# A two-layer encoder trunk: a copy goes ahead of a sigmoid in the first gate, and a weight's remainder goes behind the rotated rows in the heads

## The chip, the core and the metric

The kernel runs on one core of a Trainium2 chip. It is one program for five engines that each work through their own list in order: TensorE (PE, with its weight loads shown apart as PEld), VectorE (DVE), ScalarE (ACT), GpSimd (POOL) and SyncE (SP), which here does nothing but start DMA transfers. The engines meet only at semaphores. The metric is the device time of one launch in microseconds (us); lower is better.

## What is computed

Two layers over 512 tokens of width 1024. Layer 0 mixes tokens by neighbourhood attention, layer 1 by latent attention with a rotated key; after each mixer a gate is added that reads a per-layer embedding `p`:

```python
for i in range(DEPTH):
    xn = rmsnorm(x, norm_g[i])
    y = mixer_na(xn, ...) if i % 2 == 0 else mixer_mla(xn, ...)
    h = x + y
    gate = jax.nn.sigmoid(rmsnorm(h, ple_norm[i]) @ ple_w_gate[i])
    x = h + gate * (p[i] @ ple_w_proj[i])
return rmsnorm(x, final_norm)
```

In the latent attention a query has 64 plain and 32 rotated columns for each of 16 heads, and the scores are a plain product over all 96. All of it is float32.

## The kernel before

A float32 product is made of three products of two parts: each operand is split into a rounded part (`hi`, a copy on ACT that rounds) and a remainder (`lo`, a subtraction on DVE or POOL), and hi·hi, lo·hi and hi·lo are added in one PSUM bank. So each weight costs a load by SP, a cast on ACT and a subtraction on POOL (`load_w`, from line 70). A load takes one of three buffers `wraw`, and it can't start before the subtraction that last read that buffer is done.

**The gate of a layer** (`gate_seven`) is a 2x2 block product by seven products instead of eight, in the order 1, 7, 2, 6, 5, 3, 4 on TensorE. Each product has two halves `i` of 12 matmuls. Products 1, 7 and 6 open banks of their own (tags mm, S, T); 2 is added onto the bank of 1, products 5 and 3 onto the bank of 6, and 4 onto the bank of 7. Before product 5 writes on a bank of product 6, the sum of product 6 that stands there has to be copied out (`s6[i]`, line 649). The remainder of product 4's weight is prepared (`prep`, line 570) after the second of these copies. When a quarter of the gate is ready, `finish` (line 590) takes the sigmoid on ACT in place in the bank, multiplies by the embedding `pe` and adds to the residual `r` on DVE, and `done` (line 1052) takes the sum of squares of that half row on ACT. When both halves of 128 rows are there, `done` normalises them on DVE (`x1n`, line 1071), TensorE turns them (`ps_T`, three banks of tag T), and they are split again, `x1h` on ACT and `x1l` on DVE, into the input of layer 1. A bank of tag T is free for the next turn when both have read it.

**The heads of layer 1** (`mla_heads`) run as 64 rounds, 8 for each pair of heads `j`. A round has a score (`ps_S`, three matmuls of queries and keys), a row maximum on DVE (`mx`), an exponential on ACT, a reciprocal on DVE (`rc`), and the division of the row on POOL (`ex`, line 830). Three rounds later TensorE turns `ex` and it is split into `pt_hi` and `pt_lo`. Between the scores, `pieces(j)` puts the work for later pairs, a few matmuls at a time. For every second pair, `rope` makes 128 rows of rotated queries: its rounded part `rh` on ACT (line 771) and its remainder `rl` on POOL (line 772). SP then moves them, 32 rows at a time, into the query tiles `qe` and `qo` of the next two pairs (`move`, line 101); the third matmul of a score multiplies with the remainders, so it needs the moves of `rl`. In the odd pairs `pieces` also loads a weight (line 885): the next rotary weight in pairs 1 and 3, the embedding `p` of layer 1 (`pT`) in pair 5.

The order on each engine is set by a scheduler that runs ahead of time; `issue_after(x)` adds an edge on `x`'s own engine, so that what the block issues on that engine stands behind `x` there. It puts no semaphore.

Of the kernel before, what the change touches and what calls it, by code (L numbers as in the profile page):

```python
# [40 lines left out]
class Trunk:  # L41
# [522 lines left out]
    def gate_seven(self, pool, layer, rh, res, after):  # L564
# [4 lines left out]
        W, A, Bk, s1, s17, s6 = {}, {}, {}, {}, {}, {}  # L569
# [15 lines left out]
                    nc.gpsimd.tensor_tensor(out=lo[:, o], in0=raw[:, o], in1=hi[:, o].bitcast(F32), op=ALU.subtract)  # L585
                W[p].append((hi, lo))

        behind, loaded = [], self.last_load

        def finish(t, n, ps, o=0, wd=S, last=False):  # L590
            x = ps
# [27 lines left out]
        for k, p in enumerate(order):  # L619
            if k in (1, 2):  # L620
                prep(order[k + 3])
            if p == 7:
                self.mixed(5)
            if p == 6:
                self.mixed(3)
            x = self.X[p]
            for i in range(2):
                for o, wd in halves if i and p in (7, 4) else ((0, S),):
                    c = slice(o, o + wd)
                    if p in banks:  # L630
                        C[p, i, o] = self.psum("O" if o else banks[p])[:, :wd]
                    ps = C[home.get(p, p), i, o]
                    m = [(x[:, 2 * s + i, k * P:(k + 1) * P], W[p][k // 2][r][:, k % 2 * S + o:k % 2 * S + o + wd])
                         for c in range(2) for s, r in ((0, 0), (1, 0), (0, 1)) for k in (2 * c, 2 * c + 1)]
                    for j, (l, r) in enumerate(m):
                        with self.tc.issue_after(mm.ins):
                            mm = nc.tensor.matmul(ps, l, r, start=j == 0 and p in banks,  # L637
                                                  stop=j == 11 and p in (2, 3, 4), skip_group_check=True)
                    if p == 1:
                        s1[i] = self.temp("s1")  # L640
                        nc.scalar.activation(s1[i], ps, AF.Copy)
                    elif p == 7:
                        nc.vector.tensor_tensor(out=ps, in0=ps, in1=s1[i][:, c], op=ALU.add)
                        if o == 0:
                            s17[i] = self.temp("s17")
                        nc.scalar.activation(s17[i][:, c], ps, AF.Copy)
                    elif p == 6:
                        s6[i] = self.temp("s6")
                        copy = nc.scalar.activation(s6[i], ps, AF.Copy)
                        if i:  # L650
                            prep(order[-1], copy)
                        for (a, b, o), t in C.items():
                            if (a, b) == (7, i):
                                sub(t, t, s6[i][:, o:o + t.shape[1]])
                    elif p == 5:
                        q = self.psum("mm" if i else "T")
                        sub(q, ps, s17[i])
                        sub(ps, ps, s1[i])
                        finish(2 + i, 1, q, last=layer == 0)
                    elif p == 2:  # L660
                        finish(i, 0, ps, last=True)
                    elif p == 3:
                        finish(i, 1, ps, last=True)
                    else:
                        finish(2 + i, 0, ps, o, wd, True)
# [51 lines left out]
    def mla_heads(self, pool, xT, cT, sets, oT):  # L717


        nc, a = self.nc, self.a  # L720
# [6 lines left out]
        R, V, W_, A, PS = {}, {}, {}, {}, {}  # L727
# [14 lines left out]
            W = lambda s, k: w[s][:, o + k * P:o + (k + 1) * P]  # L742
            return [(W(r, k), (ch, cl)[s][:, 3 + k, :]) for s, r in ((0, 0), (1, 0), (0, 1)) for k in range(2)]

        def load(key, ap, n, after=None):

            with self.tc.issue_after((A.get(after) or self.last_copy).ins) if after else nullcontext():
                W_[key] = self.load_w(ap, n, parts=2)

        def load_qr(g, after=None):  # L750
            load(("qr", g), a["mla_qr"][g], 384, after)

        def load_kv(g, after=None):
            load(("kv", g), a["mla_kv"][g], 1024, after)
# [101 lines left out]
        def pieces(j):  # L856

            n, g = j + 1, j // 2 + 1
            w = [[] for i in range(8)]
            add = lambda i, f, *x: w[i].append(lambda: f(*x))  # L860
# [13 lines left out]
            if j % 2 == 0 and j < 6:  # L874
                add(4, load_qn, g, ("k", n))
                add(5, rope, g, 0, 1)
                add(6, rope, g, 1, 5)
                add(7, rope, g, 5, 9)
                add(7, load_kv, g, ("r", g))
            elif j == 6:  # L880
                add(4, load, "w0", a["proj"][1, 0], 1024, ("q", n))
                add(6, ple)
                add(7, ple)
            elif j < 7:
                add(2, *((load_qr, g + 1, ("q", n)) if j < 5 else (load, "p", a["pT"][1], 1024, ("q", n))))
                for t in range(NT):
                    add(6 + t // 2, values, g, t)
            else:
                add(0, load, "w1", a["proj"][1, 1], 1024, "latest")
                for i in (0, 1, 2, 3, 3, 4, 5, 6, 7, 7):  # L890
                    add(i, ple)
# [20 lines left out]

        zs = self.z_phase(a["mla_z"], xT, range(NEARLY))
        load_qr(0)
        late = []
        W_["kv", 0] = self.load_w(a["mla_kv"][0], 1024, parts=2, rest=nc.vector, late=late)
# [8 lines left out]
        for i in range(70):  # L925
# [13 lines left out]
            if i == 53:  # L939
                last = self.last_mm  # L940
# [279 lines left out]
```

## Time and profile before

| what | value |
|---|---|
| median of 3 runs | 660.94 us (660.82 to 661.03) |
| the profiled execution | 660.64 us, of which the span from first to last instruction is 658.4 us |
| TensorE matmuls | 647.0 us busy, 98% of the span |
| TensorE weight loads (overlap the matmuls) | 550.6 us, 84% |
| ACT | 439.1 us, 67% |
| POOL | 432.7 us, 66% |
| DVE | 402.1 us, 61% |
| mean granted TensorE clock | 0.995 |

All times on the time axis are from the start of the span. In the timeline a row has a start, a duration, the engine, the line of the kernel, the operation and its tiles; "[0.61 <-ACT s L649]" means that the engine was idle for 0.61 us before it, until ACT finished `s` of line 649. Matmuls are pipelined, so a row's duration overlaps the next one's: the distance between starts is the pace. The first gate lies at about 294 to 322 us, the heads at about 408 to 560 us.

### The profile page before, as it was taken

The numbers are of one execution on the slowest core, as the hardware profiler recorded it, in microseconds if no ns is written. First come the engines' busy times: TensorE is split into PE (matmuls) and PEld (weight loads), VectorE is DVE, ScalarE is ACT, GpSimd is POOL, SyncE is SP. The second block draws the span as 40 slices with busy tenths as digits, with TensorE's granted clock in tenths as the row PEclk, the third lists the DMA queues.
The fourth block names the chain that finished last, engine by engine and source line by source line (L and its number), as shares of the span: only waits on it lengthen the run. The fifth ranks groups of instructions, "written<-read, shape, count | busy, mean of one in ns | idle before, by whom it ended". The sixth has DMA issues, their size and how long they took to land.

```text
span 658.4 us, 10122 instructions
## 1 busy us (share of the span) xinstructions
PE 647.0 (98%) x3419; PEld 550.6 (84%) x3419; DVE 402.1 (61%) x856; ACT 439.1 (67%) x875; POOL 432.7 (66%) x381
## 2 busy tenths in 40 slices
PE   9999999999999999999999999999999999999994
PEld 6888888998988888887899888888888888888884
DVE  6290365845656516568834613888888886474855
ACT  7672586767767743787543635897979897537945
POOL 0495475895685673787554526785959878436974
PEclk9999999999999999999999999999999999999998
DMA  9944354987575989444733334120212213583524
GB/s 320 354 143 147 98 198 122 250 221 166 190 175 181 199 192 348 157 155 158 246 86 118 103 102 148 53 76 6 64 52 66 66 65 128 205 306 128 171 86 159
DMA packets 44755, 102.18 MB, mean 155 GB/s; under 512 B 4640, under 2 KB 17696, under 8 KB 44704
## 3 DMA queue, kind: packets, MB, share of 16 engines
q1 hardware_dynamic: 33776, 83.97, 38.0%
q0 software_dynamic: 10496, 16.78, 11.7%
q10 hardware_dynamic: 432, 0.79, 0.3%
q8 instruction: 27, 0.44, 0.3%
q14 instruction: 24, 0.20, 0.1%
HBM read 89.99 MB, written 25.17 MB: 175 GB/s over the span
## 4 chain that ended last, share of the span: by engine, by line
PE 92%; DVE 2%; ACT 2%; DMA 1%; issue 1%; POOL 1%; POOLq 0%; ACTq 0%
PE ps_mm L107 35%; PE ps_S L107 13%; PE ps_mm L734 7%; PE ps_T L139 6%; PE ps_O L845 5%; PE ps_T L637 4%; PE ps_T L107 3%; PE ps_O L107 3%; PE ps_T L238 2%; PE ps_O L400 2%; PE ps_S L637 2%; PE ps_mm L637 2%; PE ps_mm L184 2%; PE ps_T L388 2%; PE ps_S L352 1%; PE ps_S L351 1%
## 5 line engine op out<-in xcount | busy, mean ns | idle before, releaser
L84 POOL TENSOR_TENSOR wwlo<-wraw,wwhi 128x1024 fp32r<-128x1024 f32 (+5 forms) x78 | 143.3, 1852 | 74.7 <-ACT wwhi L83 53.2
L83 ACT ACTIVATE wwhi<-wraw 128x1024 fp32r<-128x1024 f32 (+5 forms) x81 | 65.5, 832 | 57.3 <-issue 19.2
L585 POOL TENSOR_TENSOR wlo<-wraw,whi 128x512 fp32r<-128x512 f32 x56 | 74.0, 1356 | 24.7 <-ACT whi L583 14.9
L830 POOL TENSOR_TENSOR ex<-ex,rc 128x512 f32<-128x512 f32 x64 | 66.1, 1043 | 25.1 <-DVE rc L829 18.1
L828 ACT ACTIVATE ex<-ps_S,mx 128x512 f32<-128x512 f32 x64 | 44.0, 687 | 12.1 <-DVE mx L826 11.1
L826 DVE TENSOR_REDUCE mx<-ps_S 128x1 f32<-128x512 f32 x64 | 43.7, 682 | 7.1 <-PE ps_S L107 6.5
L96 DVE TENSOR_TENSOR pt_lo<-ps_T,pt_hi 128x512 fp32r<-128x512 f32 x64 | 43.2, 681 | 7.6 <-ACT pt_hi L94 7.3
L374 POOL TENSOR_TENSOR ex<-ex,rc 128x128 f32<-128x128 f32 (+1 forms) x64 | 36.0, 619 | 15.0 <-DVE rc L370 15.0
L94 ACT ACTIVATE pt_hi<-ps_T 128x512 fp32r<-128x512 f32 x64 | 37.7, 594 | 4.2 <-PE ps_T L139 3.9
L107 PE MATMUL ps_mm<-xh,wwhi 128*128 128x512 f32 x152 | 40.3, 398 | 0.0
L107 PE MATMUL ps_mm<-xl,wwhi 128*128 128x512 f32 x152 | 38.4, 391 | 0.0
L139 PE MATMUL ps_T<-ident,ex 128*128 128x128 f32 x256 | 38.4, 272 | 0.0
L107 PE MATMUL ps_mm<-xh,wwlo 128*128 128x512 f32 x152 | 38.2, 391 | 0.0
L139 PEld LDWEIGHTS ps_T<-ident,ex 128*128 128x128 f32 x256 | 31.4, 140 | 7.7 <-POOL ex L830 0.4
L107 PEld LDWEIGHTS ps_mm<-xh,wwlo 128*128 128x128 f32 x152 | 28.3, 188 | 5.9
L107 PEld LDWEIGHTS ps_mm<-xl,wwhi 128*128 128x128 f32 x152 | 28.3, 188 | 5.7
L583 ACT ACTIVATE whi<-wraw 128x1024 fp32r<-128x1024 f32 x28 | 29.2, 1055 | 4.9 <-DMA wraw<-sum 2.7
L205 DVE TENSOR_TENSOR u<-ps_O,u 64x512 f32<-64x512 f32 x32 | 22.0, 687 | 17.2 <-ACT u L204 16.7
L368 ACT ACTIVATE ex<-ex,mx 128x128 f32<-128x128 f32 (+1 forms) x64 | 30.3, 476 | 2.7 <-DVE mx L358 1.8
L209 POOL TENSOR_TENSOR u<-u,z 128x512 f32<-128x512 f32 x16 | 21.9, 1368 | 15.2 <-DVE u L205 10.0
L107 PEld LDWEIGHTS ps_mm<-xh,wwhi 128*128 128x128 f32 x152 | 27.3, 188 | 4.8
L107 PE MATMUL ps_S<-ke,qe 96*128 96x512 f32 x96 | 29.0, 408 | 0.3 <-DMA qe<-rl 0.3
(432 smaller groups left out, 1847.0 us busy)
## 6 DMA issues: line engine op xcount, KB each, us to landing
sum<-gate POOLq DMA_DIRECT2D x12, 1024.0 KB, 8.2
wraw<-na_qk SPq DMA_DIRECT2D x16, 512.0 KB, 3.3
wraw<-sum SPq DMA_DIRECT2D x16, 512.0 KB, 3.3
pe<-pe SPq DMA_DIRECT2D x31, 256.0 KB, 6.4
wraw<-gate SPq DMA_DIRECT2D x12, 512.0 KB, 3.3
wraw<-na_v SPq DMA_DIRECT2D x8, 512.0 KB, 4.1
sum<-sum POOLq DMA_DIRECT2D x4, 1024.0 KB, 10.7
wraw<-na_o SPq DMA_DIRECT2D x8, 512.0 KB, 4.4
```

The costliest lines, as they stand in the source:

```text
L83: nc.scalar.activation(hi[:, c], raw[:, c], AF.Copy)
L84: f = lambda e, c=c: e.tensor_tensor(out=lo[:, c], in0=raw[:, c], in1=hi[:, c].bitcast(F32), op=ALU.subtract)
L94: self.last_copy = nc.scalar.activation(hi, src, AF.Copy, scale=scale)
L96: nc.vector.tensor_tensor(out=lo, in0=src, in1=hi.bitcast(F32), op=ALU.subtract)
L107: last = self.last_mm = nc.tensor.matmul(out, l, r, start=i == 0, stop=i == n - 1)
L139: self.last_mm = self.nc.tensor.transpose(t[:, i * P:(i + 1) * P], b, self.ident)
L585: nc.gpsimd.tensor_tensor(out=lo[:, o], in0=raw[:, o], in1=hi[:, o].bitcast(F32), op=ALU.subtract)
L637: mm = nc.tensor.matmul(ps, l, r, start=j == 0 and p in banks, stop=j == 11 and p in (2, 3, 4), skip_group_check=True)
L734: self.last_mm = nc.tensor.matmul(PS[key], *terms[i], start=i == 0, stop=i == len(terms) - 1)
L826: nc.vector.reduce_max(mx, sp, axis=AX.X, negate=True)
L828: nc.scalar.activation(ex, sp, AF.Exp, bias=mx, accum_out=sm)
L830: nc.gpsimd.tensor_tensor(out=ex, in0=ex, in1=rc.to_broadcast([P, S]), op=ALU.mult)
```

## The change

Two places. In the gate of layer 0 only, the second half of product 2 is no longer finished where it is computed; it is held back until the first copy of product 6 has been issued, and its `finish` is put behind that copy. In the heads, the three loads of the odd pairs get a second edge: what they issue on POOL (the weight's two subtractions) is put behind the remainder `rl` of the rotated rows of the same group.

```diff
@@ gate_seven
-        behind, loaded = [], self.last_load
+        behind, held, loaded = [], [], self.last_load
...
                     elif p == 6:
                         s6[i] = self.temp("s6")
                         copy = nc.scalar.activation(s6[i], ps, AF.Copy)
+                        if held:
+                            with self.tc.issue_after(copy.ins):
+                                finish(*held.pop(), last=True)
...
+                    elif p == 2 and i and layer == 0:
+                        held.append((i, 0, ps))
                     elif p == 2:
                         finish(i, 0, ps, last=True)
@@ mla_heads
-        def load(key, ap, n, after=None):
+        def load(key, ap, n, after=None, rests=None):
             with self.tc.issue_after((A.get(after) or self.last_copy).ins) if after else nullcontext():
-                W_[key] = self.load_w(ap, n, parts=2)
-
-        def load_qr(g, after=None):
-            load(("qr", g), a["mla_qr"][g], 384, after)
+                with self.tc.issue_after(A[rests].ins) if rests else nullcontext():
+                    W_[key] = self.load_w(ap, n, parts=2)
+
+        def load_qr(g, after=None, rests=None):
+            load(("qr", g), a["mla_qr"][g], 384, after, rests)
...
-                add(2, *((load_qr, g + 1, ("q", n)) if j < 5 else (load, "p", a["pT"][1], 1024, ("q", n))))
+                add(2, *((load_qr, g + 1, ("q", n), ("rl", g)) if j < 5 else
+                         (load, "p", a["pT"][1], 1024, ("q", n), ("rl", g))))
```

TensorE's list is the same in both, row for row. The first place is ACT's list in the first gate (`X_` is an operand of product 3, `s_` with L649 the copies of product 6, L592 a sigmoid, L1057 the sum of squares, L583 the casts of product 4's weight). Before:

```order
L646 ACTIVATE s_3177<-ps_S 128x512
L592 ACTIVATE ps_mm<-ps_mm,rs 128x512
L533 ACTIVATE X_3232<-b 128x512
L592 ACTIVATE ps_mm<-ps_mm,rs 128x512
L1057 ACTIVATE sq,ss<-r 128x512
L649 ACTIVATE s_3250<-ps_T 128x512
L649 ACTIVATE s_3266<-ps_T 128x512
L583 ACTIVATE whi<-wraw 128x1024 x2
```

And now:

```order
L646 ACTIVATE s_3177<-ps_S 128x512
L592 ACTIVATE ps_mm<-ps_mm,rs 128x512
L533 ACTIVATE X_3222<-b 128x512
L649 ACTIVATE s_3240<-ps_T 128x512
L592 ACTIVATE ps_mm<-ps_mm,rs 128x512
L1064 ACTIVATE sq,ss<-r 128x512
L649 ACTIVATE s_3266<-ps_T 128x512
L583 ACTIVATE whi<-wraw 128x1024 x2
```

The first copy has moved ahead of the second sigmoid and of the sum of squares; the second copy and the casts stand where they stood. On DVE the subtraction that uses the first copy moved with it, ahead of that sigmoid's product.

The second place is POOL's list in the heads, around the remainder `rl` of the last rotated rows (L772 before, L778 now; L84 is a weight's subtraction, here of `pT`). Before:

```order
L770 TENSOR_TENSOR rl<-rh,rl 128x512
L830 TENSOR_TENSOR ex<-ex,rc 128x512
L84 TENSOR_TENSOR wwlo<-wraw,wwhi 128x512 x2
L830 TENSOR_TENSOR ex<-ex,rc 128x512 x2
L772 TENSOR_TENSOR rl<-rl,rh 128x512
L830 TENSOR_TENSOR ex<-ex,rc 128x512
```

And now:

```order
L776 TENSOR_TENSOR rl<-rh,rl 128x512
L836 TENSOR_TENSOR ex<-ex,rc 128x512 x3
L778 TENSOR_TENSOR rl<-rl,rh 128x512
L84 TENSOR_TENSOR wwlo<-wraw,wwhi 128x512 x2
L836 TENSOR_TENSOR ex<-ex,rc 128x512
L209 TENSOR_TENSOR u<-u,z 128x512
```

The two subtractions of `pT` went from two places ahead of `rl` to right behind it. The same happened with the rotary weight of pair 3 (two subtractions of 128x192); the one of pair 1 stood behind its `rl` already and stays.

The third place is SP's list for the same rotated rows (3520 to 3523 are the tiles of the next pair, 3528 to 3531 of the pair after). Before:

```order
L101 DMA qe_3520<-rh 32x512
L101 DMA qo_3522<-rh 32x512
L101 DMA qe_3528<-rh 32x512
L82 DMA wraw<-mla_o 128x1024
L101 DMA qo_3530<-rh 32x512
L101 DMA qe_3521<-rl 32x512
L101 DMA qo_3523<-rl 32x512
```

And now:

```order
L101 DMA qe_3520<-rh 32x512
L101 DMA qo_3522<-rh 32x512
L101 DMA qe_3528<-rh 32x512
L101 DMA qe_3521<-rl 32x512
L101 DMA qo_3523<-rl 32x512
L101 DMA qe_3529<-rl 32x512
L101 DMA qo_3530<-rh 32x512
```

The moves of the remainder for the next pair now come ahead of the first load of the output weight `mla_o` and of a move for the pair after. The load of `pT` itself, which SP issued ahead of five moves of the rotated rows before, now stands behind them.

## The prediction

> **What bounds the kernel now.** I read the page's first part, then what TensorE waited for, then the timeline around each wait.
>
> ```profile
> PE 647.0 (98%) x3419; PEld 550.6 (84%) x3419; DVE 402.1 (61%) x856; ACT 439.1 (67%) x875; POOL 432.7 (66%) x381
> PE ps_T L637 <- ACT s L649: 0.6, 1, 0.6
> PE ps_mm L107 <- ACT x1h L94: 0.4, 1, 0.4
> PE ps_S L107 <- DMA qe<-rl: 0.3, 1, 0.3
> PEld ps_S L107 <- DMA qe<-rl: 1.0, 2, 0.8
> PEld ps_T L139 <- POOL ex L830: 0.4, 1, 0.4
> ```
>
> TensorE sets the end: 98% of the span, and no other engine above 67%. Time can be won only where TensorE stands, and the waits by engine name three such places of any size in the middle of the kernel. The change goes for the first (the copy of product 6) and the third (the moves of `rl`). It takes no matmul away. So the most that it can give is the length of these stands, and idle time in a row is less than that, because a matmul's duration covers part of the gap behind it; I measure from start to start.
>
> **First gate: what is removed.**
>
> ```profile
> 301.08 0.61 PE L637 MATMUL ps_T<-wlo,X 128*128 128x512 f32 x2
> 303.53 1.07 PE L637 MATMUL ps_T<-whi,X 128*128 128x512 f32 x4
> 304.43 0.61 PE L637 MATMUL ps_T<-wlo,X 128*128 128x512 f32 x2
> 305.66 1.20 PE L637 MATMUL ps_T<-whi,X 128*128 128x512 f32 x4 [0.61 <-ACT s L649]
> 306.69 0.62 PE L637 MATMUL ps_T<-wlo,X 128*128 128x512 f32 x2
> 303.07 0.63 ACT L533 ACTIVATE X<-b 128x512 fp32r<-128x512 f32 x1 [0.32 <-DVE b L557]
> 303.61 0.64 ACT L592 ACTIVATE ps_mm<-ps_mm,rs 128x512 f32<-128x512 f32 x1
> 304.40 0.63 ACT L1057 ACTIVATE sq<-r 128x512 f32<-128x512 f32 x1
> 305.03 1.06 ACT L649 ACTIVATE s<-ps_T 128x512 f32<-128x512 f32 x2
> ```
>
> Four matmuls take 304.43 - 303.53 = 0.90 us, 0.225 each. After the pair at 304.43 the next should start at 304.88; it starts at 305.66, 0.78 late. It also starts with no weight loaded ahead: its group of four takes 306.69 - 305.66 = 1.03 instead of 0.90, another 0.13. The stand costs **0.91 us**. The bank that it waits for was full at 301.69 (the row of 301.08 and its 0.61), but ACT took the cast at 303.07, the sigmoid of product 2 and a sum of squares first. In the new list the copy follows the cast: it takes the sigmoid's slot at 303.61 and, at half of 1.06, ends by about 304.2. That is 0.7 ahead of 304.88. Product 5's weight is split by then: POOL had nothing left to do for 3.25 us before 307.17, so all weights up to product 3's were done by 303.92 (that row stands below). So nothing takes the place of this wait there.
>
> What is late next on ACT: the held sigmoid starts about 0.5 later, the sum of squares 0.3 later, and DVE takes the subtraction of the copy before the sigmoid's product. Neither reaches TensorE: product 5 has two halves of 12 x 0.225 = 2.7 us each, and the second needs only the second copy, near 305.9.
>
> **First gate: what is given back.** The lead of 0.91 has to survive the passage into layer 1, where the normalised rows come from a chain that does not hang on TensorE alone.
>
> ```profile
> 307.17 5.05 POOL L585 TENSOR_TENSOR wlo<-wraw,whi 128x512 fp32r<-128x512 f32 x4 [3.25 <-issue]
> 312.25 0.33 SPq L82 DMA_DIRECT2D wraw<-mla_c  x1
> 314.15 0.66 ACT L592 ACTIVATE ps_T<-ps_T,rs 128x512 f32<-128x512 f32 x1 [0.37 <-PE ps_T L637]
> 314.74 0.62 ACT L1057 ACTIVATE sq<-r 128x512 f32<-128x512 f32 x1
> 315.81 0.85 ACT L83 ACTIVATE wwhi<-wraw 128x768 fp32r<-128x768 f32 x1 [0.36 <-DMA wraw<-mla_c]
> 321.40 1.41 DVE L1071 SCALAR_TENSOR_TENSOR x1n<-r,rs,gn 128x512 f32<-128x512 f32 x2
> 323.92 1.28 DVE L96 TENSOR_TENSOR x1l<-ps_T,x1h 128x512 fp32r<-128x512 f32 x2
> 322.12 1.47 PE L139 MATMUL ps_T<-ident,x1n 128*128 128x128 f32 x12
> 324.97 0.60 PE L139 MATMUL ps_T<-ident,x1n 128*128 128x128 f32 x4
> ```
>
> Read from the top: POOL ends product 4's subtractions at 312.22, which frees a load buffer; SP issues a load of layer 1's weight at 312.25; ACT waits for it until 315.81. Everything behind that cast on ACT, and through it on DVE (`x1n` at 321.40, `x1l` at 323.92), keeps its time although TensorE is earlier. This chain starts with the casts of product 4's weight, behind the second copy. With ACT's own distances (copy 0.53, half of 1.06; sigmoid 0.59, from 314.15 to 314.74; sum of squares 0.63, from 304.40 to 305.03) the second copy starts at 303.61 + 0.53 + 0.59 + 0.63 = 305.36, where it was 305.03 + 0.53 = 305.56. So the chain gains 0.20, against TensorE's 0.91.
>
> TensorE reaches the first turns at 322.12 - 0.91 = 321.21. Their third block needs `x1n` of the second row block, first half ready at 321.40 + 0.70 - 0.20 = 321.90; TensorE wants it after eight turns, at about 322.1: in time, barely. The next four turns, at 324.97 before, would come at 324.06, but they reuse the first of three tag-T banks, which DVE reads for `x1l` until 323.92 + 0.64 - 0.20 = 324.36. So TensorE stands again, for **0.30**. The bounds are 0 (the load lands early, or the chain moves along) and 0.65 (the load lands 0.3 later, because the embedding's load, tied to TensorE, moves toward it). I take the worked-out value, since each piece of it has a row.
>
> Net of this place: 0.91 - 0.30 = 0.61, between 0.26 and 0.91.
>
> **Heads: what is removed.**
>
> ```profile
> 515.34 0.94 PE L107 MATMUL ps_S<-ko,qo 128*128 128x512 f32 x3
> 516.12 0.65 PE L107 MATMUL ps_mm<-wwhi,cT 128*128 128x256 f32 x4
> 517.91 0.71 PE L107 MATMUL ps_S<-ke,qe 96*128 96x512 f32 x2
> 518.97 0.50 PE L107 MATMUL ps_S<-ke,qe 96*128 96x512 f32 x1 [0.34 <-DMA qe<-rl]
> 519.30 0.40 PE L734 MATMUL ps_mm<-cT,wwhi 128*128 128x512 f32 x1
> 509.37 1.03 POOL L830 TENSOR_TENSOR ex<-ex,rc 128x512 f32<-128x512 f32 x1
> 510.37 2.55 POOL L84 TENSOR_TENSOR wwlo<-wraw,wwhi 128x512 fp32r<-128x512 f32 x2
> 512.88 2.04 POOL L830 TENSOR_TENSOR ex<-ex,rc 128x512 f32<-128x512 f32 x2
> 514.87 1.30 POOL L772 TENSOR_TENSOR rl<-rl,rh 128x512 fp32r<-128x512 f32 x1
> 514.89 0.53 SPq L82 DMA_DIRECT2D wraw<-mla_o  x1
> 516.69 0.54 SPq L101 DMA_DIRECT2D qe<-rl  x1
> DMA to landing us min/median/max: 1.9/2.0/2.2
> 511.68 0.14 DVE L829 RECIPROCAL rc<-sm 128x1 f32<-128x1 f32 x1
> 511.94 0.63 ACT L771 ACTIVATE rh<-rl 128x512 fp32r<-128x512 f32 x1
> ```
>
> A score behind turns takes 516.12 - 515.34 = 0.78 to the next matmul; the one at 517.91 takes 519.30 - 517.91 = 1.39. The stand costs **0.61 us**. The move that it waits for was issued at 516.69, behind a remainder that POOL finished at 516.17 and behind a load and a move on SP.
>
> Now POOL does `ex`, `ex` and `rl` without the 2.55 between them. The second of these `ex` waits for `rc` (511.82), so it ends near 512.9; `rh` is ready at 512.57; `rl` runs from 512.9 to 514.2 instead of 514.87 to 516.17. On SP its move now follows the three moves of `rh`, the last of which was through at 514.8 (the load behind it went at 514.89). It is issued near 514.9, 1.8 earlier, and lands 2.0 later at 516.9; the third matmul wants it near 518.4. The wait is gone with 1.5 to spare, and 1 if the landing is a half slower. I take the full 0.61.
>
> What is paid: the 2.55 now lie behind `rl`, until 516.75, and the next `ex`, which followed the old `rl` at about 516.15, starts 0.6 later and ends near 517.8. Its turns are due at about 518.9 once the stand is gone, so 1.1 us cover it. `pT` itself is first used six rounds into pair 6, which begins with the score at 517.91, and the load buffer that it frees goes to an output weight, which is used when the heads end. So its later remainder and its later load cost nothing; without that cover they would cost up to the 2.55.
>
> **Small ones.** The weight load waited for `rl` a second time (1.0 less 0.8 = 0.2), at the rotated rows before these, where `rl` also moves ahead of two small subtractions; and a turn waited for `ex` (0.4 of PEld time), in a stretch where the new list has one `ex` ahead of the gate's product. Bounds 0 and 0.3; I take 0.14, about half.
>
> **The sum.** 0.61 + 0.61 + 0.14 = 1.36. The profiled execution was 660.64: 659.28. It lies 0.30 under the median of 660.94, so for a median **659.6 us**, 0.2% less.
>
> One page speaks for more. The Trainium skill, "TensorE: Matmul & The Clock Gate", section "A second HAM failure mode: psum-queue depth-cycling", holds that frequent short idling between groups makes TensorE's clock drop and be earned again, so a stand would cost more than its length. The trace does not bear it out:
>
> ```profile
> 304.00:307.00 3.00, 2.39 (x11) 1.67 (x10) 3.00 (x7) 2.85 (x7) 0.00 (x0) 1.00 0.60 175
> 508.00:523.00 15.00, 14.65 (x90) 12.53 (x89) 12.51 (x25) 12.71 (x28) 14.67 (x14) 1.00 0.25 72
> ```
>
> These are the busy times of PE, PEld, DVE, ACT and POOL in the two stretches with the stands; the granted clock is 1.00 in both.
>
> **The rivals.**
>
> *Nothing is given back* in the passage: 0.91 + 0.61 + 0.14 = 1.66, so 659.3. For it: DVE and ACT have gaps there. Against it: the cast at 315.81 waits for a load, not for TensorE.
>
> *More is given back, or one stand stays.* With the bound 0.65 of the passage and nothing from the small ones, 0.26 + 0.61 = 0.87: 660.1. If instead the move of `rl` still came late (SP's list stuck behind the earlier moves), 0.61 + 0.14 = 0.75: 660.2. That is the case in which the second half of the change does not do what it says; POOL's and SP's new lists speak against it.
>
> *Slower.* POOL was busy 14.67 of 15 us from 508 to 523. `rl` now stands ahead of `pT`'s work and waits for `rh` from ACT; if `rh` comes late, POOL stands, and every `ex` behind it, now with 2.55 of subtractions in front, is late too. The cover is 0.33 (512.9 less 512.57) before `rl` slips and then 1.1 before TensorE does. From about 1.4 late it costs TensorE one for one; at 3.9 late, 2.5 us, which turns 1.36 into -1.1: 662.1. Against it: `rh` stands where it stood on ACT, and nothing ahead of it there is later.
>
> **How the numbers follow.** Forecast 659.6: 0.50. Nothing given back, 659.3: 0.18. More given back or a stand left, 660.1 to 660.2: 0.24. Slower, about 662: 0.08. What this kernel's measurement can tell from no change is about 0.2%, 1.32 us, or 659.62: the forecast sits on that edge, so I split it in halves. Faster: 0.25 + 0.18 + 0.03 (a small part of the third) = 0.46; slower 0.08; the same 0.46. The range: 659.0 (all bounds good: 0.91 + 0.61 + 0.30 = 1.82, so 659.1, and 0.1 of the runs' spread) to 660.6 (0.26 and 0.14 with the second stand left, 0.40: 660.54). The slower rival and a little more stay outside.
>
> **What would show it.** TensorE's waits lose the rows for `s` of line 649 and for `qe<-rl`; the first matmul of product 5 follows within 0.3 us of the last of product 6. In the passage a wait of the turns for `x1l` of about 0.3 appears, and the cast behind the load of `mla_c` stays at its time less 0.2. `rl` of the last rows starts some 1.9 us ahead of the place it had, measured from the score before it. Wrong would be: a wait for `ex` in 515 to 525, a third cast whose load lands later, or a lead that is gone before the heads begin.

## The result, and the profile after

| | before | after |
|---|---|---|
| median | 660.94 us (660.81 to 661.04, 7 runs) | 658.66 us (658.40 to 659.07, 7 runs) |
| the profiled execution | 660.64 us | 658.60 us |
| its span | 658.4 us | 656.6 us |

The change makes the kernel faster by 2.28 us: the ratio is 0.9966, with a 95% interval of 0.9954 to 0.9978, so the gain is 1.5 to 3.0 us. The forecast was a gain of 1.36 us, to 659.6, in a range that began at 659.0. The direction was right, and the gain was larger than the range allowed.

The engines' busy times, and waits of PE and PEld (the weight loads) in the kernel after (us in total, times, longest):

```profile
PE 646.7 (98%) x3419; PEld 550.9 (84%) x3419; DVE 401.1 (61%) x856; ACT 439.3 (67%) x875; POOL 433.0 (66%) x381
PE ps_mm L107 <- ACT x1h L94: 0.4, 1, 0.4
PEld ps_mm L107 <- ACT x1h L94: 0.9, 2, 0.7
PEld ps_T L139 <- DVE x1l L96: 0.8, 2, 0.4
```

The rows for `s` of line 649 and for `qe<-rl` are gone, and so are PEld's for the two `ex`. Behind the first weights one row has grown: the turns wait for `x1l` twice now (0.8), where it was once (0.4). That is the place where the prediction gave 0.30 back.

The first gate, on PE and ACT (start, duration, engine and line, operation):

```profile
303.37 1.08 PE L637 MATMUL ps_T<-whi,X 128*128 128x512 f32 x4
304.28 0.61 PE L637 MATMUL ps_T<-wlo,X 128*128 128x512 f32 x2
304.74 1.07 PE L637 MATMUL ps_T<-whi,X 128*128 128x512 f32 x4
305.64 0.61 PE L637 MATMUL ps_T<-wlo,X 128*128 128x512 f32 x2
303.44 0.58 ACT L649 ACTIVATE s<-ps_T 128x512 f32<-128x512 f32 x1
303.92 0.65 ACT L592 ACTIVATE ps_mm<-ps_mm,rs 128x512 f32<-128x512 f32 x1
304.48 0.63 ACT L1064 ACTIVATE sq<-r 128x512 f32<-128x512 f32 x1
305.10 0.60 ACT L649 ACTIVATE s<-ps_T 128x512 f32<-128x512 f32 x1
```

The first copy ends at 304.02, and product 5 begins at 304.74, 0.46 after the last pair of product 6 began: two matmuls at the usual 0.23. Its group of four takes 0.90, so its weight was loaded ahead again. Both parts of the 0.91 are gone.

The passage into layer 1, on SP, ACT, DVE and PE:

```profile
311.84 0.33 SPq L82 DMA_DIRECT2D wraw<-mla_c  x1
315.28 0.85 ACT L83 ACTIVATE wwhi<-wraw 128x768 fp32r<-128x768 f32 x1 [0.67 <-DMA wraw<-mla_c]
323.40 1.28 DVE L96 TENSOR_TENSOR x1l<-ps_T,x1h 128x512 fp32r<-128x512 f32 x2
321.06 1.47 PE L139 MATMUL ps_T<-ident,x1n 128*128 128x128 f32 x12
324.14 0.66 PE L139 MATMUL ps_T<-ident,x1n 128*128 128x128 f32 x4
```

The first turns come 1.06 earlier than before (322.12), the fourth group only 0.83 (324.97): the group waits until the first `x1l`, with half of 1.28, has ended at 324.04. The third cast, which the prediction put 0.20 earlier, came 0.53 earlier (315.28 for 315.81), 0.12 of it from the start of the matmuls (in the table below).

The heads, on POOL, SP and PE:

```profile
511.13 1.04 POOL L836 TENSOR_TENSOR ex<-ex,rc 128x512 f32<-128x512 f32 x1 [0.58 <-DVE rc L835]
512.13 1.29 POOL L778 TENSOR_TENSOR rl<-rl,rh 128x512 fp32r<-128x512 f32 x1
513.38 2.53 POOL L84 TENSOR_TENSOR wwlo<-wraw,wwhi 128x512 fp32r<-128x512 f32 x2
513.95 0.53 SPq L101 DMA_DIRECT2D qe<-rl  x1
514.50 0.94 PE L107 MATMUL ps_S<-ko,qo 128*128 128x512 f32 x3
517.08 0.94 PE L107 MATMUL ps_S<-ke,qe 96*128 96x512 f32 x3
517.85 0.39 PE L739 MATMUL ps_mm<-cT,wwhi 128*128 128x512 f32 x1
```

The move of `rl` is issued 0.55 ahead of the score at 514.50; before it was issued 1.35 behind that score (516.69 and 515.34). That is 1.90 earlier. The score of the next pair takes 0.77 to the next matmul, so its stand is gone.

**Step by step.** TensorE's list is the same in both kernels, 3419 matmuls in the same order. So the n-th matmul of one trace can be set against the n-th of another, each counted from the first matmul of its trace, and the lead can be read off at each place. In us, plus is ahead of the first profile before:

| profile | start (to 8 us) | gate | passage | near 481 | at 518.97 | 534 to 540 | at the end |
|---|---|---|---|---|---|---|---|
| after | +0.12 | +0.91 | -0.28 | +0.06 | +0.61 | +0.37 | 1.78 |
| forecast | | +0.91 | -0.30 | | +0.61 | +0.14, with 481 | 1.36 |

The three large terms were right to 0.02 in this profile. The small ones (0.06 near 481 and 0.37) were three times as large. The 0.12 at the start lies ahead of everything the change touches.

### The profile page after: what moved, and what is told of

Its sections match the earlier page's. It is cut to its first block, busy times and chain, and to the rows that moved or that the text cites. A ratio compares the mean times of both kernels' runs of the same rounds, so it can differ in the third digit from the quotient of the medians.

```text
span 656.6 us, 10122 instructions
## 1 busy us (share of the span) xinstructions
PE 646.7 (98%) x3419; PEld 550.9 (84%) x3419; DVE 401.1 (61%) x856; ACT 439.3 (67%) x875; POOL 433.0 (66%) x381
## 4 chain that ended last, share of the span: by engine, by line
PE 90%; DVE 3%; ACT 2%; DMA 1%; issue 1%; POOL 1%; POOLq 0%; ACTq 0%
PE ps_mm L107 36%; PE ps_S L107 13%; PE ps_mm L739 7%; PE ps_T L139 6%; PE ps_O L851 5%; PE ps_T L107 3%; PE ps_O L107 3%; PE ps_T L637 2%; PE ps_T L238 2%; PE ps_O L400 2%; PE ps_mm L637 2%; PE ps_mm L184 2%; PE ps_T L388 2%; PE ps_S L352 1%; PE ps_S L351 1%
## 5 line engine op out<-in xcount | busy, mean ns | idle before, releaser
L84 POOL TENSOR_TENSOR wwlo<-wraw,wwhi 128x1024 fp32r<-128x1024 f32 (+5 forms) x78 | 143.4, 1853 | 74.5 <-ACT wwhi L83 53.3
L583 ACT ACTIVATE whi<-wraw 128x1024 fp32r<-128x1024 f32 x28 | 29.2, 1056 | 5.0 <-DMA wraw<-sum 2.7
L107 PE MATMUL ps_S<-ko,qo 128*128 128x512 f32 x96 | 28.9, 409 | 0.0
```

Of the source, the lines that this page charges most:

```text
L84: f = lambda e, c=c: e.tensor_tensor(out=lo[:, c], in0=raw[:, c], in1=hi[:, c].bitcast(F32), op=ALU.subtract)
L107: last = self.last_mm = nc.tensor.matmul(out, l, r, start=i == 0, stop=i == n - 1)
```

## The experiments

In the table behind the last of them, all profiles are compared in this way.

**The kernel before again** (no edit), and **each part alone**. The gate alone is the change's hunks in `gate_seven`:

```diff
+                        if held:
+                            with self.tc.issue_after(copy.ins):
+                                finish(*held.pop(), last=True)
...
+                    elif p == 2 and i and layer == 0:
+                        held.append((i, 0, ps))
```

The heads alone are its hunks in `mla_heads`; and of these, the last pair alone:

```diff
-                add(2, *((load_qr, g + 1, ("q", n)) if j < 5 else (load, "p", a["pT"][1], 1024, ("q", n))))
+                add(2, *((load_qr, g + 1, ("q", n)) if j < 5 else
+                         (load, "p", a["pT"][1], 1024, ("q", n), ("rl", g))))
```

> The kernel before once more, nothing changed. Matmul for matmul, TensorE in the changed kernel leads the profiled execution before by 1.79 us at the end, of which 1.66 at the places of the change, 0.12 at the first weights; another 0.26 lies outside the span and 0.24 between the profiled execution before (660.64) and its median. My theory: these last three (0.62) are how executions differ from each other and how the profiled one differed from the timed ones; then this run's own executions spread over several tenths, its profile starts its first fp32 matmul 0.1 us or more away from 5.27, and its median is within 0.3 of the other one's. Rival: the kernel before always loses the 0.62 in some place that the change removed without being seen; then this run repeats 5.27 us within 0.02 and 2.24 us outside the span within 0.05, in every execution.

> Only the held sigmoid of the first gate. Theory: the stand of 0.91 us goes, the passage takes 0.27 back, so TensorE's lead is 0.9 at product 5 and 0.6 to 0.7 from the passage to the end; the median falls by 0.65 us, to about 660.3. Rival (the unseen 0.6 belongs to the gate): the lead is the same but the median falls by 1.2 us. Rival (the passage takes nothing back by itself, the lead was lost otherwise): 0.9.

> Only the edges that put the weights' remainders behind rl, in all three odd pairs. Theory: TensorE gains 0.08 near 481 us, 0.61 at 518.97 and 0.35 between 534 and 540, 1.03 in all, and the median falls by 1.0 us, to about 659.9. Rival (the unseen 0.6 belongs to the heads): 1.6 us. Rival (the 0.35 at 534 to 540 came from the earlier lead and not from the edges): 0.7 us.

> Only the edge of pair 5, the weight pT behind the last rl; pairs 1 and 3 as before. Theory: the stand at 518.97 goes (0.61) and so do the two short ones at 534.5 and 537.9 (0.35), because POOL's list behind pair 5 is what put ex late there; only the 0.08 near 481 stays. Median 0.95 us lower, 660.0. Rival: the two short stands hang on the edges of pairs 1 and 3, or on the lead; then 0.61 and 660.3.

Against 660.76 of the kernel before (33 runs, from 660.11 to 661.19):

| kernel | median, us | less by | ratio, 95% interval | lead at the end of the profile |
|---|---|---|---|---|
| again | 660.76 | 0.00 | 0.9994 to 1.0012 | 0.10 |
| gate alone | 660.05 | 0.71 | 0.9981 to 0.9999 | 0.36 |
| heads alone | 659.58 | 1.18 | 0.9974 to 0.9992 | 1.25 |
| last pair alone | 659.58 | 1.18 | 0.9974 to 0.9992 | 0.94 |

The first run answers its expectation: its executions spread from 660.54 to 661.24, and its profile began its first float32 matmul at 5.18 us, 0.09 ahead of the first one's 5.27, a little less than the 0.1 that I asked for. Neither part hides an unseen 0.6 us: the gate gives 0.71 and the heads 1.18, together 1.89. The last pair alone has the whole 0.61 at 518.97 and the whole 0.37 between 534 and 540. So the two short stands there hang on the edge of pair 5 and not on the lead from the gate. These are their rows in the kernel before, on PEld:

```profile
534.48 0.53 PEld L107 LDWEIGHTS ps_S<-ko,qo 128*128 128x128 f32 x3 [0.15 <-ACT ex L828]
537.93 0.42 PEld L139 LDWEIGHTS ps_T<-ident,ex 128*128 128x128 f32 x4 [0.41 <-POOL ex L830]
```

From start to start they cost 0.15 and 0.20 of TensorE's time. The edge reaches them because the scheduler draws the lists of ACT, DVE and POOL anew behind it. On ACT the exponential that the first stand waited for stood behind `u` of line 204 (533.65 and 533.04), and with the last pair alone it stands ahead of it (532.50 and 533.31). On POOL the `ex` that the second waited for was the first of the three at 536.84, behind the gate's product `u`. POOL before, two rows, then two of the changed kernel, whose order there is that of the last pair alone:

```profile
535.59 1.28 POOL L209 TENSOR_TENSOR u<-u,z 128x512 f32<-128x512 f32 x1 [1.67 <-DVE u L205]
536.84 3.04 POOL L830 TENSOR_TENSOR ex<-ex,rc 128x512 f32<-128x512 f32 x3
533.72 1.04 POOL L836 TENSOR_TENSOR ex<-ex,rc 128x512 f32<-128x512 f32 x1 [1.19 <-DVE rc L835]
534.72 1.29 POOL L209 TENSOR_TENSOR u<-u,z 128x512 f32<-128x512 f32 x1
```

The profile of the gate alone had a surprise. It lost 0.26 at 518.97, where it changes nothing (SP, then PE):

```profile
516.05 0.54 SPq L101 DMA_DIRECT2D qe<-rl  x1
518.58 0.50 PE L107 MATMUL ps_S<-ke,qe 96*128 96x512 f32 x1 [0.59 <-DMA qe<-rl]
```

POOL and SP had moved along with TensorE (516.05 for 516.69), but the third matmul came 2.53 after the issue, where it had been 2.28 before. The trace has the landing of this move at 2.5 us from its issue, and at 2.2 before. The stand that the change removes is no fixed length: it follows the landing of a move.

**The changed kernel again**, and three further edits of it: the fourth turn in another bank, a cast behind a sigmoid, a cast behind an operand.

```diff
-    def transposes(self, blocks):
+    def transposes(self, blocks, bank="T"):
-        t = self.psum("T")
+        t = self.psum(bank)
...
-                            b = self.transposes([xn[:, (4 * g + i) * P:(4 * g + i + 1) * P] for i in range(4)])
+                            b = self.transposes([xn[:, (4 * g + i) * P:(4 * g + i + 1) * P] for i in range(4)],
+                                                "O" if t % 2 and g else "T")
```

> The changed kernel itself once more. Alone, the gate gave 0.71 us and the heads 1.18, 1.89 together, where the changed kernel gave 2.28 against seven runs of before. Theory: the steps are 0.91 in the gate, 0.61 and 0.08 and 0.35 in the heads, 1.95 us in all, and what the passage takes back of it changes with the landing of one load (0.27 in the one profile, 0.05 in the profile of the gate alone); so 1.7 to 2.0 us here, between 658.8 and 659.1. Rival: the two places help each other, and the 2.28 stands (658.5). Rival: the passage takes its 0.3 back in most executions; then 1.65, 659.1.

> The changed kernel, with every fourth turn of the passage into layer 1 written to the bank of tag O, which stands empty there, instead of reusing a bank of tag T; the scheduler then puts that turn ahead of the first matmuls of layer 1. Theory: what the passage takes back comes through the bank that x1l still reads; with another bank there is no such wait, the lead behind the passage is at least the gate's 0.9, and the wait for x1l before the second rows (0.4) is gone too: 0.3 to 0.6 us less than the changed kernel. Rival: the bank is only the place where the lateness shows; the turn waits for x1n or the next matmul for x1h instead, and nothing is won (within 0.1).

The cast behind the sigmoid (`self.sig` keeps the sigmoid that `finish` issues):

```diff
-            ws = [self.load_w(a["mla_c"][part][c], 2 * wn, extra=c == 3) for c in range(4)]
+            ws = []
+            for c in range(4):
+                with self.tc.issue_after(self.sig[0, 1, 1].ins) if (part, c) == (0, 2) else nullcontext():
+                    ws.append(self.load_w(a["mla_c"][part][c], 2 * wn, extra=c == 3))
```

> The changed kernel, with the third cast of the weight mla_c behind the sigmoid that follows it on ACT, so that the load's landing no longer holds the chain to x1n and x1l; the scheduler then sets the turns of the passage between the matmuls in another order. Theory: the chain was late through that cast; x1l of the first rows comes 0.7 us earlier measured from the last matmul of the gate, the lead of 0.9 survives the passage, and the median is 0.2 to 0.4 us under the changed kernel's. Rival: the weight, cast later, makes its own remainder late, and the matmuls with wwlo wait for it: 0.5 us or more slower. Rival: the bank alone decides: same.

The cast behind the operand (`self.six` keeps the rounding of product 6's second operand):

```diff
+                after = self.six if (layer, p, c) == (0, 3, 1) else after
                 with self.tc.issue_after(after.ins) if after else nullcontext():
                     nc.scalar.activation(hi, raw, AF.Copy)
```

> The changed kernel, with the second cast of product 3's weight behind the rounding of product 6's second operand, instead of ahead of it. TensorE loses 0.36 and 0.27 us at 301.8 and 302.5 for this operand. Theory: a stand of this kind is worth its length, as the other was: TensorE's lead over the changed kernel is 0.55 to 0.63 at product 5, and the chain of ACT into the passage, which moves by less, takes some of it back: 0.3 to 0.6 us at the end. Rival: the copy of product 6 then ends too late for the earlier TensorE and takes the wait over: 0.2 or less at product 5.

Against 660.87 of the kernel before (16 runs):

| kernel | median, us | less by | ratio, 95% interval |
|---|---|---|---|
| changed again | 658.79 | 2.08 | 0.9958 to 0.9981 |
| turn in bank O | 658.26 | 2.61 | 0.9948 to 0.9976 |
| third cast later | 664.28 | -3.41 | 1.0038 to 1.0063 |
| operand first | 659.89 | 0.98 | 0.9978 to 0.9996 |

*Turn in bank O* takes 0.53 off the changed kernel. The fourth group of turns follows the first twelve at once, and no turn waits for `x1l`:

```profile
321.25 1.47 PE L139 MATMUL ps_T<-ident,x1n 128*128 128x128 f32 x12
322.56 0.60 PE L139 MATMUL ps_O<-ident,x1n 128*128 128x128 f32 x4
322.92 1.35 PE L107 MATMUL ps_mm<-wwhi,x1h 128*128 128x384 f32 x4
```

By 326 us the passage no longer costs 0.28 but gains 0.31, since the old wait for `x1h` shrinks too; from there to 400 us, where the turns of the second rows go to bank O as well, it gains another 0.16. So the bank is where the give-back is paid, as the prediction had it, and a part of the 0.53 is an old stand that the change had not touched.

*Operand first* won 0.43 at 301.8 and 302.5, where 0.55 to 0.63 was expected, and then lost 1.68 in the passage. DVE, ACT and PE's waits show why:

```profile
304.89 0.67 DVE L605 TENSOR_TENSOR r<-r,ps_mm 128x512 f32<-128x512 f32 x1
305.60 0.63 ACT L1067 ACTIVATE sq<-r 128x512 f32<-128x512 f32 x1 [1.23 <-DVE r L605]
306.23 0.58 ACT L652 ACTIVATE s<-ps_T 128x512 f32<-128x512 f32 x1
316.36 0.85 ACT L83 ACTIVATE wwhi<-wraw 128x768 fp32r<-128x768 f32 x1 [0.64 <-DMA wraw<-mla_c]
PE ps_T L139 <- DVE x1n L1081: 0.9, 1, 0.9
```

The scheduler had set the addition to `r` one place later on DVE. ACT's sum of squares waited 1.23 for it, the second copy came 1.13 later than after the change (306.23 for 305.10), the third cast 1.08 later (316.36 for 315.28), and TensorE stood for `x1n`. The old give-back, the 0.43 of new lead and the 1.08 of lateness make 0.28 + 0.43 + 1.08 = 1.79, where 1.68 was lost. This was not meant, but it shows that the chain the prediction drew, from the second copy by the casts of product 4, POOL and a load to the third cast and `x1n`, hands lateness on nearly one for one.

*Third cast later* was to free that chain, and came out 3.4 us slower than the kernel before and 5.5 slower than the changed kernel: rows of POOL and DVE, the group of `x1n` (duration in ns: least, median, most) and PE's waits:

```profile
317.86 2.23 POOL L84 TENSOR_TENSOR wwlo<-wraw,wwhi 128x768 fp32r<-128x768 f32 x1 [0.29 <-ACT wwhi L83]
317.65 2.99 DVE L1081 SCALAR_TENSOR_TENSOR x1n<-r,rs,gn 128x512 f32<-128x512 f32 x2
L1081 DVE SCALAR_TENSOR_TENSOR x1n<-r,rs,gn x8: 741/746/2330, 317.7 to 331.6; 128x512 f32<-128x512 f32 x8
PE ps_T L139 <- DVE x1n L1081: 2.1, 1, 2.1
PE ps_T L139 <- DVE x1l L96: 1.3, 1, 1.3
```

`x1n` did start earlier (317.65 for 318.65), but now it ran beside POOL's subtraction of that weight. One of its two halves took 2.33 us where the median is 0.75, and ended 0.55 behind POOL's 320.09. The scheduler had also put the addition that the second rows need behind it. TensorE stood for 2.1 and 1.3 us, and in the second of these stands, at 326.52, the granted clock fell to one half for 6.83 us (the rows stand at the end). My rival with the late weight was wrong in its place: no matmul waited for `wwlo`.

**Both ideas at once**, with one edge that keeps the addition to `r` where it stood:

```diff
-        (lo or nc.vector).tensor_tensor(out=t[:, 2 + i, :], in0=x, in1=t[:, i, :].bitcast(F32), op=ALU.subtract)
+        with self.tc.issue_after(self.added.ins) if (p, i, self.layer) == (3, 1, 0) else nullcontext():
+          (lo or nc.vector).tensor_tensor(out=t[:, 2 + i, :], in0=x, in1=t[:, i, :].bitcast(F32), op=ALU.subtract)
```

> Both ideas on top of the changed kernel: every fourth turn of the passage in bank O, and the second cast of product 3's weight behind the rounding of product 6's second operand; this time one more edge keeps the addition to r ahead of product 3's remainder on DVE, as it stood before, so that ACT's list differs by the place of that one cast and the lists of the other engines not at all. Theory from the run operand_first: TensorE wins 0.37 at 301.8 and 302.5, the second copy of product 6 ends at its old time (there it ended 1.1 later, behind that addition), the chain through the casts of product 4 to x1n keeps its time, and TensorE meets it at the second rows' x1n: 0.2 to 0.4 us under the run turn_in_bank_O, 658.0. Rival: the chain was already the last to arrive there, and the 0.37 is waited away: same, 658.3.

657.91 us (657.74 to 658.22, 5 runs) against 660.68 (8 runs) of before: ratio 0.9960, interval 0.9946 to 0.9974, a gain of 2.77. The lead is 0.52 at the operand, 0.91 at the gate and +0.17 in the passage, with another 0.16 by 400 us as with bank O alone. At the end of the profile it is 2.73, against 2.32 with bank O alone. The times do not separate the two: the gains are 2.77 and 2.61, each against its own runs of before, and the intervals overlap, so what the second idea adds is shown by the trace alone. Its span, 655.7, is 0.9 under that of the changed kernel, and the only wait of PE left outside the warming-up is at the first weights:

```profile
PE ps_T L968 <- PEq L1222: 0.8, 1, 0.8
PE ps_mm L465 <- ACT whi L444: 0.6, 1, 0.6
```

It has the lowest median of the versions tried.

**Further profiles of the kernel before (look 1 to 3) and of the changed kernel (changed look 1 to 3)**, with no edits.

> The kernel before, for one more profile. The spans of its timed executions have a median of 658.6 to 658.7, its two profiles so far 658.4 and 658.3, while the profiles of the changed kernel (656.6, 656.7) are at the median of its spans. Theory: executions of before differ in the stand at 518.97, which hangs on how long the move of rl takes to land: it was 0.61 and 0.66 us in the two profiles and 0.88 in the one of the gate alone; a profile whose span is near 658.7 shows it at 0.8 or more. Rival: the difference lies at the start (the first weights) and the stand is 0.61 to 0.66 in all.

> The kernel before, a second such execution, with the same expectation as the look ahead of it: a span near 658.7 goes with a stand at 518.97 of 0.8 us or more (theory), or with a late start (rival).

> The kernel before, a third such execution, with the same expectation as the look ahead of it: a span near 658.7 goes with a stand at 518.97 of 0.8 us or more (theory), or with a late start (rival).

> The changed kernel, for one more profile. Three more profiles of before (spans 658.6 to 658.8) started the regular matmuls 0.25 to 0.34 us later than the profile on which the sum was made, and lost nothing more in the heads. Theory: the start varies from execution to execution whatever the kernel; this profile shows the same steps as the two of the changed kernel so far (0.91 at the gate, 0.05 to 0.27 lost in the passage, 0.61 at 518.97, 0.3 to 0.4 from 534 to 540) and a start anywhere from 0.1 early to 0.35 late, its span 656.5 to 657.1 with it. Rival: the changed kernel starts earlier as a rule; then its start is within 0.13 of the first profile before, as in both so far, in all three looks.

> The changed kernel, a second such execution, with the same expectation: the start 0.1 early to 0.35 late (theory) or always within 0.13 of the first profile before (rival); the steps at the gate, in the passage and in the heads as before.

> The changed kernel, a third such execution, with the same expectation: the start 0.1 early to 0.35 late (theory) or always within 0.13 of the first profile before (rival); the steps at the gate, in the passage and in the heads as before.

| profile | start | gate | passage | near 481 | at 518.97 | 534 to 540 | at the end |
|---|---|---|---|---|---|---|---|
| again | +0.08 | -0.01 | -0.03 | +0.06 | -0.05 | -0.01 | 0.10 |
| look 1 | -0.30 | 0.00 | -0.01 | -0.09 | +0.05 | -0.02 | -0.40 |
| look 2 | -0.22 | +0.03 | -0.01 | -0.08 | +0.18 | -0.02 | -0.19 |
| look 3 | -0.35 | +0.04 | -0.01 | +0.07 | +0.05 | -0.02 | -0.32 |
| gate alone | -0.08 | +0.91 | -0.06 | -0.09 | -0.26 | -0.03 | 0.36 |
| heads alone | +0.19 | -0.01 | 0.00 | +0.06 | +0.61 | +0.37 | 1.25 |
| last pair alone | +0.07 | +0.01 | -0.02 | -0.10 | +0.61 | +0.37 | 0.94 |
| after | +0.12 | +0.91 | -0.28 | +0.06 | +0.61 | +0.37 | 1.78 |
| changed again | -0.01 | +0.91 | -0.14 | +0.06 | +0.61 | +0.34 | 1.76 |
| changed look 1 | -0.10 | +0.91 | -0.08 | +0.06 | +0.61 | +0.35 | 1.68 |
| changed look 2 | -0.07 | +0.91 | -0.17 | +0.06 | +0.61 | +0.36 | 1.61 |
| changed look 3 | -0.17 | +0.91 | -0.50 | +0.06 | +0.61 | +0.36 | 1.31 |

(Differences up to 0.11 between the places make up the rest of a row.)

My theory fell: the spans of 658.6 to 658.8 (looks 1 to 3) do not go with a longer stand at 518.97, which was 0.05 to 0.18 shorter there, but with a later start. The second theory held, if barely: the changed kernel, too, starts anywhere from 0.12 early to 0.17 late, and of its three looks only the third, with 0.17, lies outside the 0.13 of the rival. The column near 481 needs care: every profile with pair 3's edge has +0.06, but so do two of the six others without it, so the 0.06 is a stand that the edge takes away in those executions that have it. And the one term that varies in the changed kernel is the passage, from 0.08 to 0.50. It follows the landing of the load of `mla_c` almost one for one. From SP's issue to the cast behind it, with the landing that the trace has for this load (us from its issue):

| profile | issue | landing | cast | cast less issue | passage |
|---|---|---|---|---|---|
| gate alone | 312.15 | 3.1 | 315.33 | 3.18 | -0.06 |
| changed look 1 | 312.15 | 3.1 | 315.37 | 3.22 | -0.08 |
| changed again | 312.04 | 3.1 | 315.29 | 3.25 | -0.14 |
| changed look 2 | 312.16 | 3.2 | 315.44 | 3.28 | -0.17 |
| after | 311.84 | 3.3 | 315.28 | 3.44 | -0.28 |
| changed look 3 | 312.11 | 3.5 | 315.75 | 3.64 | -0.50 |

The last row's timeline, on SP, ACT and PE:

```profile
312.11 0.33 SPq L82 DMA_DIRECT2D wraw<-mla_c  x1
315.75 0.85 ACT L83 ACTIVATE wwhi<-wraw 128x768 fp32r<-128x768 f32 x1 [0.96 <-POOL wwlo L84]
324.61 0.65 PE L139 MATMUL ps_T<-ident,x1n 128*128 128x128 f32 x4 [0.28 <-DVE x1l L96]
```

ACT's wait is put down to POOL's subtraction there. It was the load, which landed 3.5 us after its issue, at 315.6: in the profile after, the cast started at 315.28 while that subtraction ran until 315.43, so it doesn't depend on it. Why the same load lands earlier or later is not shown.

```profile
311.75 3.68 POOL L84 TENSOR_TENSOR wwlo<-wraw,wwhi 128x768 fp32r<-128x768 f32 x2
```

## Why the prediction was right in its steps and wrong in its size

**The gate, 0.91: right.** 0.91 in every profile with this part of the change. Nothing took the place of the wait, and the copy ended 0.7 ahead of product 5, as worked out.

**The passage, -0.30: right in its mechanism, and a variable.** The turns wait for the tag-T bank that `x1l` still reads; bank O takes the wait away. That the first profile's 0.28 met the 0.30 is partly luck. The chain gained more than the 0.20 that was forecast (the second copy starts at 305.10 for 305.56, less 0.12 for the start: 0.34). So `x1l` ended at 324.04, only 0.13 behind the time at which the fourth group was due (324.97 - 1.06 = 323.91). The rest is what the sum left out here: 0.10 from the end of `x1l` to the turn at 324.14, and about 0.05 because the group then took 0.41 instead of 0.35 to the next matmul, as in the first gate the group behind the stand took longer. What I treated as one value with bounds of 0 and 0.65 goes with the landing of a load: -0.08, -0.14, -0.17, -0.28 and -0.50 in five profiles, -0.23 in the mean.

**The heads, 0.61: right.** 0.61 in every profile with the edge of pair 5. `rl` starts 0.11 behind the score before it (512.13 and 512.02), where it was 2.01 (514.87 and 512.86): 1.90 earlier, as forecast. The rival in which POOL stands for `rh` did not come about: `rl` follows the `ex` ahead of it at once (512.13, with that `ex` from 511.13 for 1.04).

**The small ones, 0.14: the term that was mis-sized.** This is the step of the sum that failed. The place was right (POOL's new list has one `ex` ahead of the gate's product), the size was not: they measured 0.06 and 0.36, 0.42 together. I had read PEld's row for POOL's `ex` (0.4), which is worth 0.20 from start to start, and halved it with the other; the row below it in the same view, of the kernel before, worth 0.15, I left out:

```profile
PEld ps_S L107 <- ACT ex L828: 0.2, 1, 0.2
```

Both stands lay behind the place where the scheduler's list changed, so both were to be asked for one by one. This term's upper bound, 0.30, was too low as well, and with it the range's lower end.

So the steps sum to 0.91 - 0.23 + 0.61 + 0.06 + 0.36 = 1.71 in the mean of five profiles, where 1.36 was forecast: 0.28 of the difference from the small ones, 0.07 from the passage. That sum alone gives 660.94 - 1.71 = 659.2, still inside the range. What took the median out of it is the rest, and there the second step failed: the 0.1 that the range left for the runs' spread.

**The rest, 2.28 less 1.71.** Part of this 0.57 is scatter between executions. The kernel before had medians of 660.94, 660.76, 660.87 and 660.68 in four sets of runs, the changed one 658.66 and 658.79: the gain is 1.9 to 2.3 by the pair that is taken, and the first result took the highest and the lowest. Two pieces can be named. The start of the matmuls lies 0.05 late in the mean of the five profiles of the changed kernel, and 0.16 late in the five of before: 0.11, ahead of everything that the change touches. What lies outside the span is 2.16 us in the median of 33 runs of before, and 2.01 and 2.08 in those of the changed kernel: about 0.1. Neither is shown to be the change's doing. The remaining 0.2 to 0.4 lies within the interval and its cause stays open. My range allowed only 0.1 for scatter; the start alone takes several times that.

In the latest starts the cause is the clock. The first regular matmuls of the first profile of before, and of look 3:

```profile
5.27 0.49 PE L465 MATMUL ps_mm<-whi 128*128 128x512 f32 x1 [0.47 <-ACT whi L444]
5.60 0.40 PE L465 MATMUL ps_mm<-wlo,whi 128*128 128x512 f32 x1
```

```profile
5.30 0.80 PE L465 MATMUL ps_mm<-whi 128*128 128x512 f32 x1
5.90 0.63 PE L465 MATMUL ps_mm<-wlo,whi 128*128 128x512 f32 x1
```

In the second the same matmuls take 0.80 and 0.63, as if at half speed. The trace's record of the clock gives full speed from 3.81 us of the span in the one and from 6.72 in the other; over all profiles compared here it begins anywhere between 3.4 and 6.7 us, whatever the kernel. The Trainium skill, "TensorE: Matmul & The Clock Gate", section "What's actually happening", says that the clock is released after a busy window of about 3.4 us, and that this window runs freely and isn't reset by the start of a kernel. The traces agree: the spread is 3.3 us.

The clock is not the whole of the start. In the three profiles where full speed begins at 6.41 to 6.72, behind the first regular matmuls, the start is 0.22 to 0.35 late. Where it begins at 5.41 or earlier, the start still lies between 0.17 late (changed look 3) and 0.19 early (heads alone): there the first regular matmul itself came at 5.43 and at 5.07, in the first of the two after a wait of 0.40 for its weight.

The rule of that page of the Trainium skill which the prediction weighed and set aside, that frequent short idling makes the clock drop, stays set aside for stands like these: in all profiles of the changed kernel the mean granted clock is 0.996 or 0.997. With stands of 2.1 and 1.3 us close together, *third cast later* shows the drop.

## What to carry to other kernels

Read every wait behind the place where a scheduler's list changes, however small, and price each from start to start: here the two smallest rows held 0.36 of the 1.71 us that the steps show. A lead that a local fix gives is worth as much as the next chain that doesn't hang on the same engine lets through; if that chain ends in a buffer's reuse, another buffer can be worth more than the chain's own speed (0.53 us here). Before a difference of 0.2 us is explained, take several profiles of the same kernel: this one's start moves by 0.4 without any change.

## What the runs showed of the hardware

- The granted clock changes on a grid of 3.413 us: in *third cast later* it was at full for 320.85 us (94 times 3.413) and then at one half for 6.83 (twice), and the first stretch of full clock lasts 648.53 or 645.12 us (190 or 189 times) in the other runs. It fell although TensorE was not idle: in the 3.41 us ahead of the drop it was busy for 1.62. In *operand first*, with 2.25 busy in one such step (322.44 to 325.85), it stayed at full.

```profile
323.11:326.52 3.41, 1.62 (x8) 0.99 (x8) 3.10 (x6) 2.42 (x6) 1.75 (x4) 1.00 0.58 229
326.52:329.93 3.41, 2.30 (x9) 2.33 (x10) 3.30 (x6) 1.18 (x3) 0.00 (x0) 0.50 0.13 53
```

- A DVE operation on two SBUF operands (`x1n`) can stand until a POOL subtraction beside it is done: in *third cast later* one took 2.33 us for 0.75, while POOL's took 2.23 for 1.86. In the other 16 profiles no weight's subtraction ran beside an `x1n` there, and each took 0.74 to 0.75. The Trainium skill, "SBUF — State Buffer", section "SBUF: two separate sides", describes the ports that the two engines share as an exclusive lock held for a whole instruction; the trace agrees.
- The same load, issued at the same place, let the cast behind it go between 3.18 and 3.64 us after its issue, and the move of `rl` let its matmul go 2.28 or 2.53 us after its issue. Wherever such a landing ends a wait, a price from one profile has some 0.2 us of scatter.
